# Two FFN ends of a two-layer diffusion backbone on one Trainium2 core: the last product's operands placed ahead of norm steps, the second end pinned to source order, and four residual buffers

## The chip, the cores and the metric

The kernel runs on one core of one Trainium2 chip. The metric is the device time of one execution in microseconds (us); a row of runs is given by its median. The engines are named as in the profile: PE is TensorE, DVE is VectorE, ACT is ScalarE, POOL is GpSimd, SP is SyncE, which issues most of the loads and stores. All arithmetic is float32; a matmul of two float32 operands is done as three passes over their high and low parts.

## The reference, cut to what matters

Two layers run over 512 latent tokens and 256 context tokens of 1024 columns. Each layer has a mixer and a SwiGLU FFN, and each of the two is wrapped in the same way:

```python
def _rms(x, gain, eps=1e-6):
    y = x * lax.rsqrt(jnp.mean(x * x, axis=-1, keepdims=True) + eps)
    return y * gain

def _swiglu(h, w_gate, w_up, w_down):
    return (jax.nn.silu(h @ w_gate) * (h @ w_up)) @ w_down
...
h_lat = _modulate(_rms(x_lat, norm_pre_ffn[l]), m_lat[3], m_lat[4])
x_lat = x_lat + m_lat[5] * _rms(_swiglu(h_lat, w_gate[l], w_up[l], w_down[l]), norm_post_ffn[l])
```

`m_lat` are the six parts of `silu(c) @ mod_w[l] + mod_b[l]`. In layer 0 the context tokens go through the same steps. In layer 1 only the latent tokens do, and `x_lat` behind its FFN is the output.

## The kernel before

Tokens are handled in tiles of 128: t = 0 to 3 latent, 4 and 5 context. The FFN of layer 0 runs over six tiles in the order 4, 5, 0, 1, 2, 3, the one of layer 1 over the four latent tiles.

**The down product** (`down`, L1706) uses a scheme of seven block products in place of eight. Each product p runs over 11 row pairs of the weights in six groups: g0 holds one pair, g1 to g5 two each. `operands` (L1728) makes what one group needs: the weight block is loaded to `raw` (or lies in `t`), ScalarE casts it to its high part `wH` (L1755) and the activations to theirs, `two` or `aH` (L1756); VectorE subtracts to get the low parts, `wL` (L1757), `two` again or `aL` (L1758). `two` has two places and `aH`/`aL` is the third, so they come round every three groups; `wH` and `wL` have four buffers. `ahead(3)` keeps three groups' operands made in advance. TensorE then takes, for each of nh token tiles, three matmuls per row pair: wH by the high part, wL by the high part, wH by the low part; every matmul is recorded at L355. Layer 0 has nh = 3, layer 1 has nh = 2.

The last product (p = 6, called "12") takes its last three groups g3, g4, g5 tile by tile: first all three for tile i = 0, then for i = 1, and so on. When a product has ended for a tile, VectorE adds it to the tile's sum `y` (L1798).

**The end of a tile** is `post_pre` (L1508), a generator that runs in steps. It loads the residual `xr` (L1512); ScalarE squares `y` and sums it up (L676, to `junk` and `sq`) and VectorE makes `pn` = y times the gate row `gv` (L746); next VectorE makes `ms` (L666) and GpSimd `rs` = ms to the power -0.5 (L668); then VectorE makes xr = pn * rs + xr (L755) and SP stores it. In layer 0 the norm of the next mixer follows: a Square of xr, `ms`, `rs`, and `dg`, the identity times rs (L689). From xr and dg of a pair of tiles TensorE makes the transposed tiles `hT` (in four `turn` steps), ScalarE scales them to `hf` (L727) and casts them (L734), VectorE makes their low parts (L735). That is h1, the input of the next mixer.

`later` (L1527) files such a generator with a count that begins two behind that of the one before, and `tick` (L1532) takes one step of the one with the smallest count. Product 5 files the ends of the first nh tiles; product 6 calls `tick` once for each group and tile (L1828) and files the others. In layer 1 the very last tile (3) has its own `final` (L2117): two halves with own sums of squares, tile `xl`.

**Who sets the order.** A scheduler puts each engine's instructions in order. Matmuls are pinned to program order in these stretches. In layer 0, `order_from` (L1546) marks the beginning of product 6, and `order_to` (L1549) makes each instruction of ScalarE and VectorE between that mark and its call wait for the one before it in the source, so that these two engines run in source order. In layer 1 nothing does.

Behind the first FFN the first part of the next mixer, the value product `nat` with its operands, begins in the same stretch (`values`, L2049): `value` (L2040) loads a weight unit to `raw` (three buffers), ScalarE casts it, VectorE makes its low part (L769, L770). The unit called `wx` is needed only for the second half of the columns. Then the modulation of layer 1 is summed up from rows of mod_w (`mraw`, `macc`, L579 to L597), and TensorE sums it over partitions (`mod_acc`).

Of the kernel before, what the change touches and what calls it, by code (L numbers as in the profile page):

```python
# [316 lines left out]
class Net:  # L317
# [353 lines left out]
    def sumsq(self, src, junk=None, ss=None):  # L671
        if junk is None:
            junk = self.wp.tile([P, D], BF16, tag="mraw", bufs=2, name="junk")[:, : src.shape[-1]]
        if ss is None:
            ss = self.sm.tile([P, 1], F32, tag="ss", name="ss")
        self.nc.scalar.activation(junk, src, AF.Square, accum_out=ss)  # L676
        return ss
# [830 lines left out]
    def post_pre(self, pp, y, t, gvs, xsrc, xdst, nxt, cuts):  # L1508

        nc = self.nc  # L1510
        xt = pp.tile([P, D], F32, tag="xt", bufs=4 if nxt and isinstance(nxt[2], Split) else 2, name=f"xr{t}")
        nc.sync.dma_start(out=xt, in_=xsrc(t))  # L1512

        def store(c):
            nc.sync.dma_start(out=xdst(t)[:, c], in_=xt[:, c])

        yield from self.post_norm(y, xt, gvs[0 if t < LT else 1], cuts, xdst and store)
        if nxt is not None:
            A, B, h = nxt
            yield from self.pre_norm(pp, t, xt, A, B, h)  # L1520
# [5 lines left out]

    def later(self, steps):  # L1527

        self.steps.append([self.steps[-1][2] + 2 if self.steps else 0, steps, 0])
        self.steps[-1][2] = self.steps[-1][0]  # L1530
# [175 lines left out]
    def down(self, l, fp, qp, rp, xp, quad, early, tiles, n, ending, finish):  # L1706
# [93 lines left out]
        for p, (name, where) in enumerate(seven):  # L1800
            order = [(g, i) for g in range(ng) for i in range(nh)]
            if p == 6:
                tail = ng - 3
                order = [(g, i) for g, i in order if g < tail] + [(g, i) for i in range(nh) for g in range(tail, ng)]
            if p == 6 and not l:
                self.order_from()
            for at, (g, i) in enumerate(order):
# [19 lines left out]
                if p == 6:  # L1827
                    self.tick()  # L1828
                    if begin and (g, i) == (tail + 1, 0):
                        begin(0, 0)  # L1830
                    if begin and i and g > tail:
                        self.turn_step()
                    if begin and g >= tail and i == nh - 1:
                        begin(0, g - tail + 1)
# [13 lines left out]
                elif name == "S3":  # L1848
                    nc.scalar.copy(y1[:, low], b)
                    plus(y1[:, high], b, ALU.subtract)  # L1850
                elif name == "22":
                    plus(y1[:, low], b)
                    self.later(end(y1, t1))
                    if l and i == nh - 1:
                        close = final(dp, y0, t0)
                else:
                    plus(y0[:, low], b)
                    if l and i == nh - 1:
                        close()
                    else:  # L1860
                        self.later(end(y0, t0))
        self.pinned = pinned
        yield follow

    def run(self):
# [170 lines left out]
        def ending(dp):  # L2036
# [12 lines left out]
            def values():  # L2049
# [12 lines left out]
                for c in range(2):  # L2062
                    for x, t in enumerate(order):
# [18 lines left out]
                        if c == 0 and x == 3:  # L2082
                            self.order_to(*self.latest)
                            value(1, 0)
                        if c or x > 2:
# [18 lines left out]
        def ending(dp):  # L2104
# [12 lines left out]
            def final(pool, y, t):  # L2117

                halves = [slice(512 * i, 512 * i + 512) for i in range(2)]
                xt = ep.tile([P, D], F32, tag="xt", bufs=2, name="xl")  # L2120
                nc.sync.dma_start(out=xt, in_=xat(x1)(t))
# [10 lines left out]
                def close():  # L2132
# [4 lines left out]
                    for c in halves:  # L2137
                        nc.vector.scalar_tensor_tensor(xt[:, c], tmp[:, c], rs, xt[:, c], op0=ALU.mult, op1=ALU.add)
                        nc.sync.dma_start(out=dst(t)[:, c], in_=xt[:, c])

                return close
# [58 lines left out]
```

## Time and profile before

| | us |
|---|---|
| median of 3 runs | 1691.47 |
| lowest and highest run | 1688.34, 1691.84 |
| profiled execution, its own time | 1689.01 |
| its span, first to last instruction | 1686.9 |
| product 6 of the first FFN on TensorE begins | 885.66 |
| product 6 of the second FFN on TensorE begins | 1660.49 |
| TensorE busy | 1646.0 (98%) |
| VectorE busy | 1309.3 (78%) |
| ScalarE busy | 920.0 (55%) |

A row of a timeline gives start, duration, engine, line, operation, output <- inputs, shapes, a count, and in brackets how long the engine was idle before it and what ended that. The names of buffers stand without their numbers, so that `xr` is that of any tile. The last line of a program is that of its closing instructions.

### The profile page before, as it was taken

What the parts mean: (1) busy time and instruction counts of PE and PEld (TensorE: products, weight loads), DVE (VectorE), ACT (ScalarE), POOL (GpSimd) and SP (SyncE); (2) the same over time, 40 slices, a digit from 0 to 9 for tenths busy, and PEclk for the clock granted to TensorE, in tenths of its full rate; (3) what the DMA queues carried; (4) which work ended last, traced back from release to release, by engine and by line L of the source; (5) the groups of instructions that cost most, each with busy time, mean ns of one, the idle gap of its engine ahead of it and who ended that gap; (6) DMA issues with size and microseconds to landing.
All of it is one profiled execution on the core that took longest, in us unless ns stands there. A gap on an engine that the chain in (4) does not pass through costs nothing.

```text
span 1686.9 us, 32540 instructions
## 1 busy us (share of the span) xinstructions
PE 1646.0 (98%) x13407; PEld 1481.6 (88%) x13407; DVE 1309.3 (78%) x2105; ACT 920.0 (55%) x1560; POOL 124.4 (7%) x129
## 2 busy tenths in 40 slices
PE   7999998999999999999999999999999999999997
PEld 5889987888999999998887888888888899999875
DVE  4889768875898988878667548788774599987987
ACT  4745567836543443445447436566664565555654
POOL 1004210011000000003102000000000100000221
PEclk9999999999999999999999999999999999999999
DMA  9651002164243444348625542121124333333793
GB/s 329 192 155 41 2 27 101 51 211 152 85 140 102 148 149 140 113 149 175 131 91 197 177 125 61 51 64 39 52 65 149 125 113 114 112 101 101 190 198 137
DMA packets 184736, 204.79 MB, mean 121 GB/s; under 512 B 7142, under 2 KB 141836, under 8 KB 184588
## 3 DMA queue, kind: packets, MB, share of 16 engines
q1 hardware_dynamic: 173632, 181.82, 34.4%
q0 software_dynamic: 9024, 17.30, 5.9%
q10 hardware_dynamic: 1932, 3.59, 0.6%
q8 instruction: 105, 1.72, 0.4%
q14 instruction: 43, 0.35, 0.1%
HBM read 193.23 MB, written 9.46 MB: 120 GB/s over the span
## 4 chain that ended last, share of the span: by engine, by line
PE 83%; DVE 8%; ACT 4%; DMA 3%; issue 2%; POOL 1%; DVEq 0%; SPq 0%; POOLq 0%; ACTq 0%
PE nat L355 12%; PE a L355 11%; PE ff L355 8%; PE E L355 8%; PE x L355 7%; PE oproj L355 6%; PE b L355 4%; PE D L355 4%; PE o L355 4%; PE fq L355 3%; PE gqk L355 2%; PE pearly L355 2%; PE S L355 2%; PE poh L355 1%; PE attO L355 1%
## 5 line engine op out<-in xcount | busy, mean ns | idle before, releaser
L355 PE MATMUL nat<-wH,x 128*128 128x256 f32 (+2 forms) x968 | 225.4, 321 | 3.0 <-ACT x L734 2.6
L355 PEld LDWEIGHTS nat<-wH,x 128*128 128x128 f32 x968 | 162.2, 190 | 19.2 <-ACT x L734 3.7
L824 ACT CAST wH<-raw 128x1024 fp32r<-128x1024 f32 x120 | 125.4, 1054 | 94.7 <-DVE raw L849 31.7
L825 DVE TENSOR_TENSOR wL<-raw,wH 128x1024 fp32r<-128x1024 f32 x120 | 145.6, 1220 | 20.4 <-ACT wH L824 19.9
L355 PE MATMUL nat<-wL,x 128*128 128x256 f32 (+2 forms) x484 | 153.4, 317 | 0.3 <-DVE wL L770 0.3
L770 DVE TENSOR_TENSOR wL<-raw,wH 128x1024 fp32r<-128x1024 f32 (+1 forms) x83 | 98.7, 1197 | 46.7 <-ACT wH L769 45.8
L355 PE MATMUL ff<-x,wH 128*128 128x512 f32 (+1 forms) x512 | 127.7, 340 | 0.0
L668 POOL TENSOR_TENSOR rs<-ms,neghalf 128x1 f32<-128x1 f32 (+2 forms) x62 | 66.5, 1077 | 783.3 <-DVE ms L666 783.2
L769 ACT CAST wH<-raw 128x1024 fp32r<-128x1024 f32 (+1 forms) x83 | 85.0, 1036 | 69.8 <-PE ff L355 19.8
L355 PE MATMUL oproj<-wH,x 128*128 128x512 f32 x320 | 102.2, 395 | 0.6 <-ACT x L1290 0.6
L597 DVE SCALAR_TENSOR_TENSOR macc<-mraw,scT,macc 128x1024 f32<-128x1024 f32 x70 | 88.2, 1279 | 13.8 <-DMA mraw<-in_mod_w_dram 13.6
L355 PEld LDWEIGHTS nat<-wL,x 128*128 128x128 f32 x484 | 92.1, 190 | 6.0 <-DVE wL L770 0.7
L355 PEld LDWEIGHTS ff<-x,wH 128*128 128x128 f32 x512 | 87.3, 190 | 10.0
L355 PE MATMUL x<-wH,two 128*128 128x512 f32 x280 | 90.5, 392 | 0.9 <-DVE y L1798 0.7
L976 ACT COPY qkh<-arr 128x512 f32<-128x512 f32 x112 | 70.2, 644 | 36.2 <-DVE arr L981 32.1
L1723 POOL DMA_DIRECT2D t<-in_ffn_w_down_dram x36 | 41.8, 1225 | 648.0 <-DVE wL L1757 610.7
L355 PE MATMUL ff<-x,wL 128*128 128x256 f32 (+1 forms) x256 | 86.2, 337 | 0.0
L849 DVE TENSOR_TENSOR raw<-raw 128x512 f32<-128x512 f32 x120 | 82.7, 689 | 2.8
L981 DVE TENSOR_TENSOR arr<-arr,f 128x512 f32<-128x512 f32 x112 | 74.1, 686 | 1.9 <-ACT qkh L976 0.3
L355 PE MATMUL E<-x,wH 128*128 128x384 f32 (+1 forms) x320 | 70.9, 311 | 0.0
L355 PEld LDWEIGHTS oproj<-wH,x 128*128 128x128 f32 x320 | 59.5, 188 | 12.8 <-ACT x L1290 1.2
L355 PE MATMUL a<-x,dH 128*128 128x384 f32 (+1 forms) x320 | 70.4, 309 | 0.2 <-ACT early L897 0.2
(420 smaller groups left out, 4544.6 us busy)
## 6 DMA issues: line engine op xcount, KB each, us to landing
mraw<-in_mod_w_dram SPq DMA_DIRECT2D x80, 512.0 KB, 4.4
raw<-in_ffn_w_gate_dram SPq DMA_DIRECT2D x44, 512.0 KB, 4.9
raw<-in_ffn_w_up_dram SPq DMA_DIRECT2D x44, 512.0 KB, 4.3
raw<-in_odd_w_in_dram SPq DMA_DIRECT2D x40, 512.0 KB, 3.7
t<-in_ffn_w_down_dram POOLq DMA_DIRECT2D x30, 512.0 KB, 7.8
raw<-in_ffn_w_down_dram SPq DMA_DIRECT2D x28, 512.0 KB, 7.5
mraw<-in_mod_w_dram SPq DMA_DIRECT2D x32, 256.0 KB, 6.0
raw<-in_even_w_in_dram SPq DMA_DIRECT2D x16, 512.0 KB, 3.9
```

What stands on the lines that cost most here:

```text
L355: return self.pin(self.nc.tensor.matmul(*a, **k))
L597: nc.vector.scalar_tensor_tensor(a, u, w, a, op0=ALU.mult, op1=ALU.add)
L668: nc.gpsimd.tensor_tensor(rs, ms, self.neghalf.to_broadcast([P, w]), op=ALU.pow)
L769: nc.scalar.copy(H[:, :m], raw[:, :m])
L770: nc.vector.tensor_tensor(L[:, :m], raw[:, :m], H[:, :m].bitcast(F32), op=ALU.subtract)
L824: self.nc.scalar.copy(H, f)
L825: self.nc.vector.tensor_tensor(L, f, H.bitcast(F32), op=ALU.subtract)
L849: add = lambda o, x, y: nc.vector.tensor_tensor(o, x, y, op=ALU.add)
L976: nc.scalar.copy(qkv[:, :, :, half, :], dst)
L981: nc.vector.tensor_tensor(dst, dst, tb, op=ALU.mult)
L1723: add = lambda o, src: self.pin(nc.gpsimd.dma_start(out=o, in_=src, accum_op=ALU.add))
```

## The change

Four things are changed.

1. In product 6, `tick` is no longer called at group g2 (`tail - 1`), but for g2's first tile in layer 0; at (g3, tile 0) it is called three times in layer 0 and twice in layer 1, in place of once.
2. The marks for source order are set in layer 1 too, and `close` of the last tile now returns its last Square and its last VectorE instruction, up to which source order holds. `later` has a gap of 0 in layer 1, so that the ends of two tiles take their steps in turn.
3. The tile `xt` of the residuals has four buffers in layer 1's FFN end, in place of two.
4. In layer 0, what the unit wx issues comes behind the last VectorE instruction of h1.

```diff
@@ -673,7 +673,7 @@
             junk = self.wp.tile([P, D], BF16, tag="mraw", bufs=2, name="junk")[:, : src.shape[-1]]
         if ss is None:
             ss = self.sm.tile([P, 1], F32, tag="ss", name="ss")
-        self.nc.scalar.activation(junk, src, AF.Square, accum_out=ss)
+        self.squared = self.nc.scalar.activation(junk, src, AF.Square, accum_out=ss)
         return ss
 
     def pre_norm(self, pool, t, xt, A, B, h):
@@ -1508,7 +1508,7 @@
     def post_pre(self, pp, y, t, gvs, xsrc, xdst, nxt, cuts):
 
         nc = self.nc
-        xt = pp.tile([P, D], F32, tag="xt", bufs=4 if nxt and isinstance(nxt[2], Split) else 2, name=f"xr{t}")
+        xt = pp.tile([P, D], F32, tag="xt", bufs=2 if nxt and isinstance(nxt[2], Forms) else 4, name=f"xr{t}")
         nc.sync.dma_start(out=xt, in_=xsrc(t))
 
         def store(c):
@@ -1524,9 +1524,9 @@
         while len(self.turns) > left:
             self.turns.pop(0)()
 
-    def later(self, steps):
-
-        self.steps.append([self.steps[-1][2] + 2 if self.steps else 0, steps, 0])
+    def later(self, steps, gap=2):
+
+        self.steps.append([self.steps[-1][2] + gap if self.steps else 0, steps, 0])
         self.steps[-1][2] = self.steps[-1][0]
 
     def tick(self, n=1):
@@ -1802,7 +1802,7 @@
             if p == 6:
                 tail = ng - 3
                 order = [(g, i) for g, i in order if g < tail] + [(g, i) for i in range(nh) for g in range(tail, ng)]
-            if p == 6 and not l:
+            if p == 6:
                 self.order_from()
             for at, (g, i) in enumerate(order):
                 if p == 5 and g == ng - 2 and i == 0:
@@ -1825,7 +1825,8 @@
                 if all(x != g for x, _ in order[at + 1 :]):
                     ready.pop((p, g))
                 if p == 6:
-                    self.tick()
+                    if g != tail - 1 or i == 0 and not l:
+                        self.tick((2 if l else nh) if (g, i) == (tail, 0) else 1)
                     if begin and (g, i) == (tail + 1, 0):
                         begin(0, 0)
                     if begin and i and g > tail:
@@ -1850,15 +1851,15 @@
                     plus(y1[:, high], b, ALU.subtract)
                 elif name == "22":
                     plus(y1[:, low], b)
-                    self.later(end(y1, t1))
+                    self.later(end(y1, t1), 0 if l else 2)
                     if l and i == nh - 1:
                         close = final(dp, y0, t0)
                 else:
                     plus(y0[:, low], b)
                     if l and i == nh - 1:
-                        close()
+                        self.order_to(*close())
                     else:
-                        self.later(end(y0, t0))
+                        self.later(end(y0, t0), 0 if l else 2)
         self.pinned = pinned
         yield follow
 
@@ -2081,7 +2082,8 @@
                         self.nc.scalar.copy(fi[:, t, 512 * c : 512 * c + 512], pt[:, :512])
                         if c == 0 and x == 3:
                             self.order_to(*self.latest)
-                            value(1, 0)
+                            with self.tc.issue_after(self.latest[1].ins):
+                                value(1, 0)
                         if c or x > 2:
                             mod(2 if c or x == 3 else 3)
                 self.pinned = False
@@ -2117,7 +2119,7 @@
             def final(pool, y, t):
 
                 halves = [slice(512 * i, 512 * i + 512) for i in range(2)]
-                xt = ep.tile([P, D], F32, tag="xt", bufs=2, name="xl")
+                xt = ep.tile([P, D], F32, tag="xt", bufs=4, name="xl")
                 nc.sync.dma_start(out=xt, in_=xat(x1)(t))
                 tmp = pool.tile([P, D], F32, name="pl")
                 ss = pool.tile([P, 2], F32, name="sl")
@@ -2135,8 +2137,9 @@
                     nc.vector.tensor_reduce(s, ss, axis=AX.X, op=ALU.add)
                     rs = self.rstd(s, D)
                     for c in halves:
-                        nc.vector.scalar_tensor_tensor(xt[:, c], tmp[:, c], rs, xt[:, c], op0=ALU.mult, op1=ALU.add)
+                        r = nc.vector.scalar_tensor_tensor(xt[:, c], tmp[:, c], rs, xt[:, c], op0=ALU.mult, op1=ALU.add)
                         nc.sync.dma_start(out=dst(t)[:, c], in_=xt[:, c])
+                    return self.squared, r
 
                 return close
```

The first place is the end of the first FFN, VectorE, where g5's operands (`wL` and `aL` from `qb`) are made. The numbered xr is that of tile 5:

```order
 L1758 TENSOR_TENSOR two<-zy,two 128x768
 L689 TENSOR_SCALAR dg_9495<-ident,rs 128x128
+L1757 TENSOR_TENSOR wL<-raw,wH 128x1024
+L1758 TENSOR_TENSOR aL<-qb,aH 128x768
 L755 SCALAR_TENSOR_TENSOR xr_9451<-pn,rs,xr_9451 128x1024
 L746 TENSOR_TENSOR pn<-y_8479,gv_9347 128x1024
-L1757 TENSOR_TENSOR wL<-raw,wH 128x1024
-L1758 TENSOR_TENSOR aL<-qb,aH 128x768
 L666 TENSOR_SCALAR ms<-ss 128x1
 L666 TENSOR_SCALAR ms<-sq 128x1
```

The two low parts now stand ahead of xr of tile 5 and of the next tile's pn. ScalarE at the same place:

```order
 L1755 CAST wH<-raw 128x1024
 L1756 CAST two<-zy 128x768
+L1755 CAST wH<-raw 128x1024
+L1756 CAST aH<-qb 128x768
 L676 ACTIVATE junk,sq<-y_8479 128x1024
-L1755 CAST wH<-raw 128x1024
-L1756 CAST aH<-qb 128x768
 L676 ACTIVATE junk,ss<-xr_9451 128x1024
```

g5's two casts have moved ahead of one Square of y.

The second place is where wx's low part stood on VectorE, between tile 2's pn and the `ms` of tiles 1 and 2:

```order
 L1798 TENSOR_TENSOR y_8479<-y_8479,x_8500 128x512
 L746 TENSOR_TENSOR pn<-y_8479,gv_9347 128x1024
-L770 TENSOR_TENSOR wx<-raw,wx 128x1024
 L666 TENSOR_SCALAR ms<-ss 128x1
 L666 TENSOR_SCALAR ms<-sq 128x1
```

It now stands behind the last L735, just ahead of the first `macc`; its cast on ScalarE has not moved. On SP one load of the value product goes with it, into the loads of mod_w:

```order
 L1515 DMA x_96<-xr_9577 128x1024
-L768 DMA raw<-in_odd_w_in_dram 128x2x512 x3
+L768 DMA raw<-in_odd_w_in_dram 128x2x512 x2
 L1515 DMA x_96<-xr_9702 128x1024
 L1515 DMA x_96<-xr_9736 128x1024
 L579 DMA mraw_9940<-in_mod_w_dram 128x1024
 L579 DMA mraw_9942<-in_mod_w_dram 128x1024
+L768 DMA raw<-in_odd_w_in_dram 128x2x512
 L579 DMA mraw_9973<-in_mod_w_dram 128x1024
```

The third of three loads has moved behind two stores and two loads of mod_w.

The third place is VectorE in product 6 of the second FFN, behind g2's `aL`. Before, with xr of tiles 0 (17859) and 1 (17895):

```order
L746 TENSOR_TENSOR pn<-y_17126,gv_17797 128x1024
L666 TENSOR_SCALAR ms<-sq 128x1
L1757 TENSOR_TENSOR wL<-raw,wH 128x1024
L1758 TENSOR_TENSOR two<-qb,two 128x512
L755 SCALAR_TENSOR_TENSOR xr_17859<-pn,rs,xr_17859 128x1024
L746 TENSOR_TENSOR pn<-y_17126,gv_17797 128x1024
L1757 TENSOR_TENSOR wL<-raw,wH 128x1024
L1758 TENSOR_TENSOR two<-qb,two 128x512
L666 TENSOR_SCALAR ms<-sq 128x1
L1757 TENSOR_TENSOR wL<-raw,wH 128x1024
L1758 TENSOR_TENSOR aL<-qb,aH 128x512
L1798 TENSOR_TENSOR y_17126<-y_17126,x_17143 128x512
```

The same place with the change, where tile 1's xr is 17869:

```order
L746 TENSOR_TENSOR pn<-y_17126,gv_17797 128x1024 x2
L1757 TENSOR_TENSOR wL<-raw,wH 128x1024
L1758 TENSOR_TENSOR two<-qb,two 128x512
L666 TENSOR_SCALAR ms<-sq 128x1 x2
L1757 TENSOR_TENSOR wL<-raw,wH 128x1024
L1758 TENSOR_TENSOR two<-qb,two 128x512
L1757 TENSOR_TENSOR wL<-raw,wH 128x1024
L1758 TENSOR_TENSOR aL<-qb,aH 128x512
L755 SCALAR_TENSOR_TENSOR xr_17859<-pn,rs,xr_17859 128x1024
L755 SCALAR_TENSOR_TENSOR xr_17869<-pn,rs,xr_17869 128x1024
L1798 TENSOR_TENSOR y_17126<-y_17126,x_17143 128x512
L746 TENSOR_TENSOR pn<-y_17126,gv_17797 128x1024
```

Both pn come first, then the operands of g3, g4 and g5 with only the two small ms between them, then both xr. Behind these rows, xr of tile 2 stood last of all on VectorE, behind both halves of xl; now it stands ahead of the last tile's y. On ScalarE both Squares of tiles 0 and 1 now stand ahead of g3's cast; before, the first stood behind it and the second behind g3's `two`. On SP tile 1's residual is loaded ahead of g4's and g5's weights, tile 2's right behind them, and the two stores of xl come last.

## The prediction

> **What bounds the kernel now.** The page comes first: its span, and the chain that ended last.
>
> ```profile
> span 1686.9 us, 32540 instructions
> ...
> PE 83%; DVE 8%; ACT 4%; DMA 3%; issue 2%; POOL 1%; DVEq 0%; SPq 0%; POOLq 0%; ACTq 0%
> ```
>
> TensorE carries the chain, so a change pays only where TensorE waits, or behind its last matmul. The change touches the last product of each FFN; the timelines of these two stretches come next. First TensorE at the end of the first FFN (start, duration, and in brackets the idle time before it with what ended it):
>
> ```profile
> 898.58 0.39 PE L355 MATMUL x<-wH,aH 128*128 128x512 f32 x1
> 900.53 0.50 PE L355 MATMUL x<-wL,aH 128*128 128x512 f32 x1 [1.56 <-DVE wL L1757]
> 901.39 0.50 PE L355 MATMUL x<-wH,aL 128*128 128x512 f32 x1 [0.37 <-DVE ms L666]
> ...
> 905.18 1.05 PE L355 MATMUL hT<-dg,xr 128*128 128x128 f32 x8
> ```
>
> Group g5's second and third matmul wait for its two low parts. At TensorE's pace (0.227 us a matmul) the third would start at 899.03 and not at 901.39: 2.36 us are lost, some 2.45 with the slower pace behind a wait. Next, where TensorE waits again in this stretch, and VectorE and ScalarE around both places:
>
> ```profile
> 922.98 0.94 PE L355 MATMUL hT<-dg,xr 128*128 128x128 f32 x6 [0.92 <-DVE dg L689]
> 923.67 0.48 PE L355 MATMUL nat<-wH,x 128*128 128x512 f32 x1
> ```
>
> ```profile
> 896.40 0.29 DVE L689 TENSOR_SCALAR dg<-ident,rs 128x128 f32<-128x128 f32 x1 [0.44 <-POOL rs L668]
> 896.92 1.28 DVE L755 SCALAR_TENSOR_TENSOR xr<-pn,rs,xr 128x1024 f32<-128x1024 f32 x1 [0.23 <-POOL rs L668]
> ...
> 899.25 1.22 DVE L1757 TENSOR_TENSOR wL<-raw,wH 128x1024 fp32r<-128x1024 f32 x1
> 900.39 0.95 DVE L1758 TENSOR_TENSOR aL<-qb,aH 128x768 fp32r<-128x768 f32 x1
> ...
> 903.04 0.29 DVE L689 TENSOR_SCALAR dg<-ident,rs 128x128 f32<-128x128 f32 x1 [0.44 <-POOL rs L668]
> ...
> 919.50 1.22 DVE L746 TENSOR_TENSOR pn<-y,gv 128x1024 f32<-128x1024 f32 x1
> 920.63 1.22 DVE L770 TENSOR_TENSOR wx<-raw,wx 128x1024 fp32r<-128x1024 f32 x1
> 921.77 0.14 DVE L666 TENSOR_SCALAR ms<-ss 128x1 f32<-128x1 f32 x1
> ```
>
> ```profile
> 895.84 0.84 ACT L1756 CAST aH<-qb 128x768 fp32r<-128x768 f32 x1 [0.21 <-PE x L355]
> ...
> 898.24 1.06 ACT L676 ACTIVATE junk<-xr 128x1024 bf16<-128x1024 f32 x1 [1.56 <-DVE xr L755]
> ...
> 912.16 1.03 ACT L727 ACTIVATE hf<-hT,modcol,aff 128x256 f32<-128x256 f32 x2 [0.64 <-PE hT L355]
> ```
>
> VectorE does a norm step (xr from 896.92, and a pn) before g5's operands, although ScalarE's second half for them, aH, stands ready from 896.68. At the end of the second FFN the same shows on TensorE once, and then VectorE has the end:
>
> ```profile
> 1660.49 0.39 PE L355 MATMUL x<-wH,two 128*128 128x512 f32 x1
> ...
> 1670.34 0.51 PE L355 MATMUL x<-wL,two 128*128 128x512 f32 x1 [1.29 <-DVE wL L1757]
> ```
>
> ```profile
> 1663.27 1.22 DVE L746 TENSOR_TENSOR pn<-y,gv 128x1024 f32<-128x1024 f32 x1
> ...
> 1678.05 0.69 DVE L1798 TENSOR_TENSOR y<-y,x 128x512 f32<-128x512 f32 x1 [0.89 <-PE x L355]
> ...
> 1681.99 1.28 DVE L755 SCALAR_TENSOR_TENSOR xr<-pn,rs,xr 128x1024 f32<-128x1024 f32 x1
> ```
>
> ```profile
> 1663.24 0.61 ACT L1756 CAST two<-qb 128x512 fp32r<-128x512 f32 x1
> ```
>
> ```profile
> 1654.60 3.38 SPq L1724 DMA_DIRECT2D raw<-in_ffn_w_down_dram  x2
> ...
> 1678.51 0.32 SPq L1512 DMA_DIRECT2D xr<-x  x1
> 1681.44 1.00 SPq L2139 DMA_DIRECT2D out_dram<-xl  x2
> 1683.30 0.33 SPq L1515 DMA_DIRECT2D out_dram<-xr  x1
> ```
>
> The very last step is token tile 2's xr. Its residual is loaded only at 1678.51, since two buffers serve four tiles, and its store, issued at 1683.30, ends the program 3.6 us later.
>
> **The change, part by part.** VectorE starts an instruction some 0.08 us before the one ahead of it ends (899.25, 1.22 long, then 900.39), so I count 1.13 us for 1024 columns, 0.87 for 768, 0.60 for 512, 1.20 for xr.
>
> *First FFN, operands ahead.* After dg (896.40) wL now runs 896.61 to 897.83, aL 897.74 to 898.70. TensorE wants them at 898.81 and 899.03: both waits go, and TensorE is some 2.45 us earlier at the next group. What is late next: xr and pn stand behind the operands (898.61 and 899.81), and the Square of xr on ScalarE moves from 898.24 to 899.93 and ends at 901.1. The value unit's cast stands behind that Square, its low part (1.22) behind the cast, and dg, at 903.04 before, comes at 903.2. TensorE's first hT needs that dg: it gets there near 902.7 and goes on at about 903.5, where it went on at 905.18 before: 1.7 us are kept. The Square of y, which now waits behind aH's cast (895.84, itself waiting for TensorE), ends by 897.7, and pn wants it at 899.81: nothing.
>
> *First FFN, wx.* ScalarE's hf at 912.16 had waited for hT, so it moves with TensorE, by 1.8. Behind it the casts and low parts of the value units follow, so that pn (919.50) comes at 917.67, 1.83 earlier. Then wx, which held VectorE from 920.63 to 921.77, is gone from here: ms moves by 1.83 + 1.13 = 2.96, from 921.77 to 918.8, and the dg on which TensorE waited 0.92 us comes at 919.68. TensorE, held about half a microsecond by the last of those low parts (an estimate from the same steps), reaches this hT at 919.8. Both meet, and nat (923.67) starts 2.97 us earlier. **First term: 2.97 us.** wx's low part now stands behind the last split of h1:
>
> ```profile
> 947.05 0.69 DVE L735 TENSOR_TENSOR x<-hf,x 128x512 fp32r<-128x512 f32 x1 [1.58 <-ACT x L734]
> ```
>
> ```profile
> L355 PEld LDWEIGHTS nat<-wx,x x36: 186/188/189, 955.8 to 985.3; 128*128 128x128 f32 x36
> ```
>
> Made by 949 and wanted at 955.8 on before's clock, it costs nothing by itself. The fourth value unit's load now waits for it (its buffer is wx's raw tile), and the modulation loads queue behind it on SP; that is the rival below.
>
> *Second FFN, source order.* On ScalarE both Squares now stand ahead of g3's cast: the first takes the place where `two` stood (1663.24 is when the first Square had ended), the second ends its sum at 1664.4. g3's cast ends at 1665.34, its `two` at 1665.86, g4's at 1667.33, g5's at 1668.80. VectorE: pn 1663.27, pn 1664.42, wL 1665.55, two 1666.68, two ms, wL 1667.41, two 1668.54, wL 1669.14, aL 1670.27 to 1670.95. TensorE reaches g3 at 1667.30 (30 matmuls of 0.227 behind 1660.49), g4 at 1668.66, g5 near 1670.5; it waits 0.2 to 0.4 us for g4's low part and ends near 1676.1, not 1678.03. That alone is not the gain, because VectorE is late next. GpSimd's square root does not get in between:
>
> ```profile
> 894.04 2.84 POOL L668 TENSOR_TENSOR rs<-ms,neghalf 128x1 f32<-128x1 f32 x2 [4.67 <-DVE ms L666]
> ...
> 1664.70 2.00 POOL L668 TENSOR_TENSOR rs<-ms,neghalf 128x1 f32<-128x1 f32 x1 [31.44 <-DVE ms L666]
> ...
> 1677.31 0.55 POOL L668 TENSOR_TENSOR rs<-ms,neghalf 128x1 f32<-128x1 f32 x1 [4.22 <-DVE ms L666]
> ```
>
> Alone it takes 0.55 us (1677.31). Behind VectorE's tensor_tensor instructions it takes 2.00 and ends about 0.4 after the last of them. So the first rs, asked for at 1667.5, comes at 1671.36. Then xr 1671.39, xr 1672.59, y 1673.79, pn 1674.5, ms 1675.7, rs 1676.5, xr 1676.57, and y of the last tile at 1677.77, where it was 1678.05: 0.28 earlier, as VectorE runs in order. From here on the steps are the same: the two half stores of xl go out 0.28 earlier, the second at 1681.82 (of the two at 1681.44 it is the last third of a microsecond, 1682.10). The issues by line give the time to landing:
>
> ```profile
> out_dram<-xr SPq DMA_DIRECT2D x3, 512.0 KB, 2.6
> ...
> out_dram<-xl SPq DMA_DIRECT2D x2, 256.0 KB, 2.1
> ```
>
> A half tile lands 2.1 us after its issue, at 1683.9, where the last whole tile landed at 1683.30 + 2.6 = 1685.9; the end moves by 2.0, from 1686.9 to 1684.9. **Second term: 2.0 us**, 0.3 from VectorE, the rest because xr and its full store no longer come last: four buffers let all residuals load at 1654 to 1658.
>
> One row is missing: whether the second rs gets in while the first xr begins at the same moment. In the pair at 894.04 the second rs ended 0.52 behind the first (dg 896.40, xr 896.92), with the short dg beside it: no delay. With a whole xr beside it, it could end 0.4 behind xr: 0.5 later. I take no delay, nearest to that pair.
>
> The Trainium skill, "SBUF — State Buffer", section "SBUF: two separate sides", says that VectorE with two SBUF inputs and GpSimd share one port pair, which whoever starts first holds for its whole instruction. The 2.00 us agree with it. By it either rs or xr would wait here, so the second term would be 1.5 rather than 2.0.
>
> *Loads.* The extra residual load (512 KB) goes ahead of g4's and g5's weights on SP. In a stretch of the first FFN in which the DMA engines were full, the core moved (last two columns: share and GB/s)
>
> ```profile
> 880.00:890.00 10.00, 10.00 (x46) 8.28 (x45) 6.70 (x10) 6.16 (x8) 0.56 (x1) 1.00 0.96 372
> ```
>
> so I estimate 1.4 us for it. g5's weights, issued at 1657.6 (the second of 1654.60), are wanted at 1667.2. Hidden.
>
> **Sum.** 2.97 + 2.0 = 5.0 us. The profiled execution took 1689.01 us (span 1686.9 and 2.1 around it), so it would take 1684.0. The median of the three runs, 1691.47, lies 2.46 above it; less 5.0, it gives **1686.5**.
>
> **Rivals.**
>
> *The first FFN gives it back.* dg at 903.2 is no earlier than before. If ScalarE's chain behind it (hf, casts, Squares) doesn't move up with TensorE, only wx's 1.13 us reach the dg at 922.64. For it: VectorE was the releaser in all of these waits. Against it: hf waited 0.64 for TensorE. Then 1.1 + 2.0 = 3.1: 1688.4.
>
> *The second FFN gives nothing.* VectorE has been the bound, and pn of tile 1 and both Squares now stand ahead of three groups. If gv or a Square lands 2 us later, y of the last tile does too, and it eats the 2.0: 1688.5.
>
> *The port*, as above: 4.5, 1687.0.
>
> *The modulation loads become the bound, and it is slower.* While the value product runs, VectorE adds up rows of mod_w as they land, and TensorE reads the sum:
>
> ```profile
> 983.32 1.06 PE L355 MATMUL mod_acc<-macc,one 128*32 128x512 f32 x8
> ```
>
> ```profile
> DVE macc L597 <- DMA mraw<-in_mod_w_dram: 9.3, 7, 2.4
> ```
>
> ```profile
> 979.45 1.28 DVE L597 SCALAR_TENSOR_TENSOR macc<-mraw,scT,macc 128x1024 f32<-128x1024 f32 x1 [1.70 <-DMA mraw<-in_mod_w_dram]
> ```
>
> The sum is ready at 980.73, 2.6 us ahead. wx pushes its beginning back by 1.1 beside TensorE's gain, and the added load in the queue by some 1.4: 0.1 of slack is left. If each of the seven waits for a load grows by one load of 1.4 us, TensorE stands 9.7 us: 4.7 us slower, 1696.2. It decides from 5.1 us of added waiting. Against it: one load moves into this stretch, not seven.
>
> *It does little*: the order was already forced by buffers, within 1 us of before. The rows show the low parts waiting for nothing but VectorE's turn, which speaks against it.
>
> **How the numbers follow.** Forecast 0.50, port 0.15, first FFN gives back 0.15, second FFN gives nothing 0.11, little 0.05, slower 0.04. A measurement of this kernel can tell about 0.2%, 3.4 us, from no change: forecast and port are over it, the next three within. That is 0.65, 0.31, 0.04. The runs of before lie 3.5 us apart, the lowest 3.1 under the median, so the range goes from 1683.3 (5.0 and the lowest run) to 1690.5 (little, 1 us gained); only the slower rival is outside it, and what the scatter adds.
>
> **What will show it.** Right: no wait of TensorE at g5 in the first FFN; its first hT about 1.7 us earlier, with a new wait for dg of half a microsecond or more; nat behind the second hT 3.0 earlier; TensorE's last matmul about 1.9 earlier against that, but y of the last tile only 0.3; xl last on VectorE. Wrong: nat behind the second hT less than 2 us earlier; a wait at mod_acc; y of the last tile later relative to the product's start; a gv that lands later.

## The result, and the profile after

The changed kernel takes 1683.48 us (median of 5 runs, 1682.4 to 1685.94), the kernel before 1691.29 us (5 runs beside it): a ratio of 0.996, with a 95% interval of 0.995 to 0.9971. In a second comparison, of the same two kernels later, it was 0.996 again (0.9947 to 0.9973). The two medians lie 7.8 us apart; by the ratio it is 6.8, with an interval of 4.9 to 8.5, and the forecast was 5.0 saved.

The profiled execution took 1683.48 us, with a span of 1681.5, 5.4 less than before. From the page, the span and the shares of the chain that ended last:

```profile
span 1681.5 us, 32537 instructions
...
PE 85%; DVE 7%; ACT 3%; DMA 3%; issue 1%; POOL 0%; ACTq 0%; DVEq 0%; POOLq 0%
```

TensorE carries slightly more of the chain, VectorE slightly less. Now TensorE at the end of the first FFN, in the timeline (the first three rows are the first three of g5's six matmuls for the first tile):

```profile
897.66 0.39 PE L355 MATMUL x<-wH,aH 128*128 128x512 f32 x1
897.88 0.39 PE L355 MATMUL x<-wL,aH 128*128 128x512 f32 x1
898.11 0.39 PE L355 MATMUL x<-wH,aL 128*128 128x512 f32 x1
...
901.74 0.38 PE L355 MATMUL hT<-dg,xr 128*128 128x128 f32 x2
902.60 0.94 PE L355 MATMUL hT<-dg,xr 128*128 128x128 f32 x6 [0.48 <-DVE dg L689]
...
918.99 1.12 PE L355 MATMUL hT<-dg,xr 128*128 128x128 f32 x8
919.86 0.47 PE L355 MATMUL nat<-wH,x 128*128 128x512 f32 x1
```

The waits of 1.56 and 0.37 us at g5 are gone: its matmuls follow each other at 0.227 us. In their place stands a wait of 0.48 for dg in the first hT, behind two of its eight matmuls, and the wait of 0.92 at the later hT, just ahead of nat, is gone too. VectorE around both places:

```profile
895.48 0.29 DVE L689 TENSOR_SCALAR dg<-ident,rs 128x128 f32<-128x128 f32 x1 [0.44 <-POOL rs L668]
895.68 1.22 DVE L1757 TENSOR_TENSOR wL<-raw,wH 128x1024 fp32r<-128x1024 f32 x1
896.82 0.95 DVE L1758 TENSOR_TENSOR aL<-qb,aH 128x768 fp32r<-128x768 f32 x1
897.68 1.28 DVE L755 SCALAR_TENSOR_TENSOR xr<-pn,rs,xr 128x1024 f32<-128x1024 f32 x1
...
901.12 1.22 DVE L770 TENSOR_TENSOR wL<-raw,wH 128x1024 fp32r<-128x1024 f32 x1 [0.73 <-ACT wH L769]
902.27 0.28 DVE L689 TENSOR_SCALAR dg<-ident,rs 128x128 f32<-128x128 f32 x1
...
916.82 1.22 DVE L746 TENSOR_TENSOR pn<-y,gv 128x1024 f32<-128x1024 f32 x1
917.96 0.14 DVE L666 TENSOR_SCALAR ms<-ss 128x1 f32<-128x1 f32 x1
```

The first dg stands at 895.48 where it stood at 896.40. Product 6 already begins 0.92 earlier (884.74 for 885.66), and so does the low part in front of this dg (894.09 for 895.01), so these 0.92 us are none of the change's doing, and every distance is taken from this dg. At the end of the second FFN, VectorE:

```profile
1664.46 0.21 DVE L666 TENSOR_SCALAR ms<-sq 128x1 f32<-128x1 f32 x2
1664.58 1.22 DVE L1757 TENSOR_TENSOR wL<-raw,wH 128x1024 fp32r<-128x1024 f32 x1
1665.72 0.68 DVE L1758 TENSOR_TENSOR two<-qb,two 128x512 fp32r<-128x512 f32 x1
...
1667.45 0.68 DVE L1758 TENSOR_TENSOR aL<-qb,aH 128x512 fp32r<-128x512 f32 x1
1668.06 2.47 DVE L755 SCALAR_TENSOR_TENSOR xr<-pn,rs,xr 128x1024 f32<-128x1024 f32 x2
...
1673.22 1.28 DVE L755 SCALAR_TENSOR_TENSOR xr<-pn,rs,xr 128x1024 f32<-128x1024 f32 x1 [0.73 <-POOL rs L668]
1674.42 0.68 DVE L1798 TENSOR_TENSOR y<-y,x 128x512 f32<-128x512 f32 x1
...
1677.03 1.42 DVE L2140 SCALAR_TENSOR_TENSOR xl<-pl,rs,xl 128x512 f32<-128x512 f32 x2 [0.73 <-DMA out_dram<-xr]
```

xl is now last on VectorE, and all three xr stand ahead of the last y. (The wait ahead of xl is put down to a store, but what VectorE waits for behind ms, 1676.14, is the rs below, done at 1676.99.) GpSimd and SP in the same stretch:

```profile
1664.76 2.05 POOL L668 TENSOR_TENSOR rs<-ms,neghalf 128x1 f32<-128x1 f32 x2 [35.37 <-DVE ms L666]
...
1676.44 0.55 POOL L668 TENSOR_TENSOR rs<-ms,neghalf 128x1 f32<-128x1 f32 x1 [3.25 <-DVE ms L666]
```

```profile
1651.07 0.90 SPq L1512 DMA_DIRECT2D xr<-x  x2
...
1655.03 0.58 SPq L1512 DMA_DIRECT2D xr<-x  x1
1669.36 5.51 SPq L1515 DMA_DIRECT2D out_dram<-xr  x3
1677.81 0.99 SPq L2141 DMA_DIRECT2D out_dram<-xl  x2
```

The loads of all three residuals are issued by 1655.6, and the program ends with two half stores where a whole one stood.

To read all the runs together, the span is cut at places that every kernel has: from the first dg to nat behind the later hT (the first FFN's end), from there to the start of product 6 of the second FFN (in it lie only wx's small parts and, in e7 and e8, the moved weight loads), and from that start to the last y and to the end of the span. In microseconds, each from one profiled execution:

| kernel | dg to nat | nat to product 6 | product 6 to last y | product 6 to end |
|---|---|---|---|---|
| before | 27.27 | 736.82 | 17.56 | 26.38 |
| before, again | 27.25 | 736.61 | 17.59 | 26.40 |
| changed | 24.38 | 737.63 | 16.93 | 23.96 |
| changed, again | 24.39 | 736.41 | 17.11 | 24.15 |
| e1 first FFN alone | 24.37 | 737.13 | 17.53 | 26.34 |
| e2 second FFN alone | 27.26 | 736.93 | 16.92 | 23.95 |
| e3 wx as before | 25.54 | 737.06 | 16.93 | 23.95 |
| e4 order, two buffers | 24.41 | 735.81 | 26.48 | 33.52 |
| e5 four buffers alone | 27.29 | 738.58 | 17.92 | 24.96 |
| e6 xr beside rs | 24.40 | 737.36 | 18.03 | 25.07 |
| e7 adds later | 24.38 | 736.65 | 16.98 | 24.01 |
| e8 both of these | 24.40 | 736.27 | 17.91 | 24.94 |
| e7, again | 24.39 | 735.89 | 16.92 | 23.95 |

The first FFN gives 2.89 us and the second 2.42, together 5.3. Kernels with the same edit repeat the two end stretches within 0.06 us, but for the second end of the changed kernel's second trace, 0.2 longer, where VectorE waits 0.18 us longer for gv; the long stretch between them, and the time ahead of the first dg (895.35 to 899.20), scatter by 2.8 and 3.9 us. (In e6's 899.20 some 1.7 us are the granted clock's, by an estimate: it is 0.66 on average between 105 and 110 us there and 1.00 in the changed kernel, and 0.34 of 5 us is 1.7.) So the times of two executions can differ by more than the change is worth: the runs of before alone lie between 1686.62 and 1694.44 us.

### The profile page after: what moved, and what is told of

It reads as the page before. It is cut to its first block, busy times and chain, and to the rows that moved or that the text cites. A ratio compares the mean times of both kernels' runs of the same rounds, so it can differ in the third digit from the quotient of the medians.

```text
span 1681.5 us, 32537 instructions
## 1 busy us (share of the span) xinstructions
PE 1644.6 (98%) x13407; PEld 1481.0 (88%) x13407; DVE 1309.8 (78%) x2105; ACT 917.5 (55%) x1560; POOL 121.4 (7%) x129
## 4 chain that ended last, share of the span: by engine, by line
PE 85%; DVE 7%; ACT 3%; DMA 3%; issue 1%; POOL 0%; ACTq 0%; DVEq 0%; POOLq 0%
PE nat L355 13%; PE a L355 12%; PE ff L355 8%; PE E L355 8%; PE x L355 7%; PE oproj L355 6%; PE o L355 4%; PE D L355 4%; PE b L355 4%; PE fq L355 3%; PE gqk L355 2%; PE pearly L355 2%; PE S L355 2%; PE poh L355 1%; PE attO L355 1%
## 5 line engine op out<-in xcount | busy, mean ns | idle before, releaser
L355 PE MATMUL b<-x,wH 128*128 128x384 f32 (+1 forms) x320 | 70.5, 309 | 0.0
```

The costliest lines, as they stand in the source:

```text
L355: return self.pin(self.nc.tensor.matmul(*a, **k))
```

## The experiments

The theory is the prediction's: two independent terms, operands ahead and wx away in the first FFN, and in the second the buffers, which take xr and its full store from the end, with a little of VectorE's order. One thing in the new trace spoke against plain adding: of the 2.89 us that TensorE was ahead at nat, 0.81 were missing at product 6. It waits in the second FFN's product that the trace calls q: first to last start of its 66 matmuls took 16.35 us, where 65 steps of 0.2266 are 14.73. One of these waits is

```profile
1608.40 0.49 PE L355 MATMUL q<-wL,aH 128*128 128x512 f32 x1 [0.24 <-DVE wL L1757]
```

and from the start at 1607.14 to the one at 1609.34 four steps take 2.20 us where 0.91 would do. ScalarE, in front of VectorE there, waits for weights:

```profile
1602.00 1.05 ACT L1755 CAST wH<-raw 128x1024 fp32r<-128x1024 f32 x1 [4.01 <-DMA raw<-in_ffn_w_down_dram]
...
1606.04 1.05 ACT L1755 CAST wH<-raw 128x1024 fp32r<-128x1024 f32 x1 [2.47 <-DMA raw<-in_ffn_w_down_dram]
```

So a rival stood beside the theory: the weight loads of the second FFN take back part of whatever the first one gains.

### e1: the first FFN alone

Against the kernel before:

```diff
-                    self.tick()
+                    if l or g != tail - 1 or i == 0:
+                        self.tick(nh if not l and (g, i) == (tail, 0) else 1)
...
-                            value(1, 0)
+                            with self.tc.issue_after(self.latest[1].ins):
+                                value(1, 0)
```

> Only the first FFN is changed (low parts of g5 ahead of the norm steps, wx behind h1); the second FFN stays as before, with two residual buffers. Theory A (the terms simply add up): nat behind the second hT comes 2.9 us earlier against dg of the first norm step than in before, and product 6 of the second FFN begins 2.9 us earlier too; time 2.9 us under before. Theory B (the second FFN's down product is bound by its weight loads): nat comes 2.9 us earlier, but TensorE then waits some 0.8 us for a low part wL in the product recorded as q, 48 us ahead of product 6, and only 2.1 us are left at product 6 and at the end. Theory C (the first FFN gives nothing by itself): under 1 us at nat.

Measured: 0.9974 of before (0.9965 to 0.9984), 4.4 us by the ratio with 2.7 to 5.9 as its interval. From dg to nat 24.37 us, 2.90 less than before. The first term stands. TensorE loses 1.6 us in q (16.31), as the rival says, and the long stretch is 0.31 longer than before's, between theory A (nothing) and B (0.8).

### e2: the second FFN alone

Against the changed kernel:

```diff
-                    if g != tail - 1 or i == 0 and not l:
-                        self.tick((2 if l else nh) if (g, i) == (tail, 0) else 1)
+                    if not l or g != tail - 1:
+                        self.tick(2 if l and (g, i) == (tail, 0) else 1)
...
-                            with self.tc.issue_after(self.latest[1].ins):
-                                value(1, 0)
+                            value(1, 0)
```

> Only the second FFN's end is changed (source order, gap 0, no tick at g2, four buffers). The recorded working: y of the last tile 0.28 us earlier against the start of product 6, the end 2.0 us earlier against that start. By the trace of the changed kernel it should be 0.63 at y and 2.4 at the end. If the port held GpSimd's second root back, 1.5. At q there should be no new wait, since TensorE comes there no earlier than before.

Measured: 0.9984 (0.9975 to 0.9993), 1.2 to 4.2 us. From product 6 to the last y 0.64 us less than before, to the end 2.43 less: the trace of the changed kernel to a hundredth. The product of the ratios of e1 and e2 is 0.9958, beside the changed kernel's 0.996: the parts add. And in q:

```profile
1611.55 0.49 PE L355 MATMUL q<-wL,aH 128*128 128x512 f32 x1 [0.24 <-DVE wL L1757]
```

the same wait (1.6 us lost in q, 16.31), in a kernel with the first FFN of before. No new wait was expected there; that there is one speaks against the rival.

### e3: wx as before

Against the changed kernel:

```diff
-                            with self.tc.issue_after(self.latest[1].ins):
-                                value(1, 0)
+                            value(1, 0)
```

> The changed kernel, with the unit wx issued where it was before. The recorded working gives wx 1.13 us of the first term: nat behind the second hT 1.1 us later than in the changed kernel, with a wait of TensorE for dg of about 0.9. Rival: TensorE comes to this hT with dg ready anyway or is held by the value product's own low parts, and wx is worth under 0.3 us. Third: since the weight loads of the second FFN take 0.8 us back anyway, nat is 1.1 us later but the start of product 6 only 0.3.

Measured: 0.9971 (0.9959 to 0.9982), not to be told from the changed kernel. In the trace it can be told. TensorE, and VectorE ahead of it:

```profile
920.83 0.94 PE L355 MATMUL hT<-dg,xr 128*128 128x128 f32 x6 [0.92 <-DVE dg L689]
921.52 0.47 PE L355 MATMUL nat<-wH,x 128*128 128x512 f32 x1
```

```profile
918.48 1.22 DVE L770 TENSOR_TENSOR wx<-raw,wx 128x1024 fp32r<-128x1024 f32 x1
919.62 0.15 DVE L666 TENSOR_SCALAR ms<-ss 128x1 f32<-128x1 f32 x1
...
920.49 0.28 DVE L689 TENSOR_SCALAR dg<-ident,rs 128x128 f32<-128x128 f32 x1 [0.67 <-POOL rs L668]
```

The wait of 0.92 is back to the hundredth, and nat comes 25.54 us behind the first dg, 1.16 later than in the changed kernel. So wx is worth 1.16 of the first term, and the operands ahead 1.73. The third theory, that only 0.3 of it would be left at product 6, can't be read from a stretch that scatters by more.

### e4: source order with two buffers

Against the changed kernel:

```diff
-        xt = pp.tile([P, D], F32, tag="xt", bufs=2 if nxt and isinstance(nxt[2], Forms) else 4, name=f"xr{t}")
+        xt = pp.tile([P, D], F32, tag="xt", bufs=4 if nxt and isinstance(nxt[2], Split) else 2, name=f"xr{t}")
...
-                xt = ep.tile([P, D], F32, tag="xt", bufs=4, name="xl")
+                xt = ep.tile([P, D], F32, tag="xt", bufs=2, name="xl")
```

> The changed kernel with two residual buffers in the second FFN in place of four. xl and tile 0 hold both, so tile 1's residual loads only behind tile 0's store (1669.4 + 2.6 + 3.3 = 1675.3) and tile 2's behind tile 1's store (1676.5 + 2.6 + 3.3 = 1682.4). Theory A (source order makes every later y wait for these loads): the end some 9 us later than in the changed kernel, 1692 to 1694, slower than before. Theory B (the order alone is the gain, buffers only help): the last y as in the changed kernel and the end within 2 us of it.

Measured: 1.0019 (1.001 to 1.0028), slower than before, although its first FFN gains as the changed kernel's does. From product 6 to the end 33.52 us, 9.56 more than in the changed kernel. VectorE and SP:

```profile
1674.05 1.28 DVE L755 SCALAR_TENSOR_TENSOR xr<-pn,rs,xr 128x1024 f32<-128x1024 f32 x1 [6.05 <-DMA xr<-x]
1675.25 0.68 DVE L1798 TENSOR_TENSOR y<-y,x 128x512 f32<-128x512 f32 x1
...
1681.42 1.28 DVE L755 SCALAR_TENSOR_TENSOR xr<-pn,rs,xr 128x1024 f32<-128x1024 f32 x1 [4.12 <-DMA xr<-x]
1682.62 0.68 DVE L1798 TENSOR_TENSOR y<-y,x 128x512 f32<-128x512 f32 x1
```

```profile
1668.02 0.36 SPq L1515 DMA_DIRECT2D out_dram<-xr  x1
1670.67 0.34 SPq L1512 DMA_DIRECT2D xr<-x  x1
1675.36 0.34 SPq L1515 DMA_DIRECT2D out_dram<-xr  x1
1677.99 0.32 SPq L1512 DMA_DIRECT2D xr<-x  x1
```

Each of these residuals is loaded some 2.6 us behind the store of the one before it, and each xr waits for that load with the next tile's y queued behind it. Source order, with the ticks and the gap that go with it, costs 7.1 us against before; it needs the four buffers. (No run takes pinning, ticks and gap apart.)

### e5: four buffers alone

Against the kernel before:

```diff
-        xt = pp.tile([P, D], F32, tag="xt", bufs=4 if nxt and isinstance(nxt[2], Split) else 2, name=f"xr{t}")
+        xt = pp.tile([P, D], F32, tag="xt", bufs=2 if nxt and isinstance(nxt[2], Forms) else 4, name=f"xr{t}")
...
-                xt = ep.tile([P, D], F32, tag="xt", bufs=2, name="xl")
+                xt = ep.tile([P, D], F32, tag="xt", bufs=4, name="xl")
```

> The kernel before with four residual buffers in the second FFN's end and nothing else. The residuals then load early, and tile 2's xr stands ahead of the last y by the scheduler's own choice. Theory A (the recorded working: 0.3 us of the second term from VectorE's order, the rest from xr and its full store no longer being last): 1.7 to 2.1 us of the 2.43 us that the second FFN's part gives between the start of product 6 and the end. Theory B (the order carries it): under 0.5 us, since the xr that is now ahead of the last y pushes it back.

Measured: 0.9991 (0.9982 to 1.0), by time not to be told from before. From product 6 to the end 24.96 us, 1.42 less than before. VectorE:

```profile
1674.72 1.28 DVE L755 SCALAR_TENSOR_TENSOR xr<-pn,rs,xr 128x1024 f32<-128x1024 f32 x1 [0.44 <-POOL rs L668]
...
1678.69 1.28 DVE L755 SCALAR_TENSOR_TENSOR xr<-pn,rs,xr 128x1024 f32<-128x1024 f32 x1 [0.73 <-POOL rs L668]
1679.90 0.68 DVE L1798 TENSOR_TENSOR y<-y,x 128x512 f32<-128x512 f32 x1
```

Nearer to theory A than to B, under its lower end: tile 2's xr, now ahead of the last y, puts that y 0.36 us later (17.92 for 17.56) and the end keeps 1.42 of the 2.43. With four buffers, the order (pinning, ticks and gap) then adds 1.0: the last y goes from 17.92 to 16.92.

### e6: xr beside rs

Against the changed kernel:

```diff
-                    if g != tail - 1 or i == 0 and not l:
-                        self.tick((2 if l else nh) if (g, i) == (tail, 0) else 1)
+                    if l and g >= tail - 1:
+                        self.tick((1 if g == tail else 0) if i == 0 else 0 if g < tail else 2 if g == ng - 1 else 1)
+                    elif g != tail - 1 or i == 0:
+                        self.tick(nh if (g, i) == (tail, 0) else 1)
```

> The changed kernel with tile 1's xr moved on VectorE behind tile 2's ms, so that it runs while GpSimd makes tile 2's rs (in the changed kernel VectorE stands idle there for 0.73 us). Theory A (the two share a port, and VectorE starts first): rs takes about 1.6 us and ends some 0.4 us behind xr; the last y is at most 0.1 us earlier against the start of product 6. Theory B (no hindrance): rs takes 0.55 to 0.61 us, VectorE does not wait, the last y and the end come 0.5 us earlier.

Measured: 0.9975 (0.9967 to 0.9984); the last y and the end are 1.1 us later against product 6 than in the changed kernel, worse than either theory. VectorE and GpSimd:

```profile
1672.96 0.69 DVE L1798 TENSOR_TENSOR y<-y,x 128x512 f32<-128x512 f32 x1
1674.87 1.22 DVE L746 TENSOR_TENSOR pn<-y,gv 128x1024 f32<-128x1024 f32 x1 [1.22 <-ACT junk L676]
1676.01 0.14 DVE L666 TENSOR_SCALAR ms<-sq 128x1 f32<-128x1 f32 x1
1676.07 1.27 DVE L755 SCALAR_TENSOR_TENSOR xr<-pn,rs,xr 128x1024 f32<-128x1024 f32 x1
1677.79 1.28 DVE L755 SCALAR_TENSOR_TENSOR xr<-pn,rs,xr 128x1024 f32<-128x1024 f32 x1 [0.44 <-POOL rs L668]
```

```profile
1676.30 1.46 POOL L668 TENSOR_TENSOR rs<-ms,neghalf 128x1 f32<-128x1 f32 x1 [5.97 <-DVE ms L666]
```

On the port, theory A holds: xr began 0.23 us ahead of rs, and rs, 0.55 us alone, took 1.46 and ended at 1677.76, 0.42 behind xr's end at 1677.34. So nothing was won here by work of VectorE beside rs. The rest was overlooked: pn and the Squares' junk share two buffers, tile 1's pn holds one until its xr is done, and tile 2's pn waited 1.22 us for the Square to leave the other.

### e7 and e8: the accumulating loads spread out

GpSimd's queue loads some weight blocks so that they are added to what the tile `t` holds; these are the accumulating loads. Against the changed kernel:

```diff
-            v.tensor_tensor(L, src, H.bitcast(F32), op=ALU.subtract)
+            split = v.tensor_tensor(L, src, H.bitcast(F32), op=ALU.subtract)
...
-            elif name == "N3":
-                add(t3(i), B(1, 1, i))
-            elif name == "SN":
-                add(t(i), B(1, 0, i))
+            elif name == ("SN" if l else "N3"):
+                behind(add(t3(i), B(1, 1, i)), split)
+            if name == ("S3" if l else "SN"):
+                behind(add(t(i), B(1, 0, i)), split)
```

Here `behind` makes the load wait, in layer 1, for the low part named. e8 is e7 with e6's edit.

> The changed kernel with the accumulating weight loads of the second FFN spread out: those issued by GpSimd during the product recorded as q (loads of its own on SP) wait until the next product's low parts, and those of that product until the one behind it. Theory A (in q the transfers of both queues compete, so that raw lands late): the 0.75 us that TensorE waited in q in the changed kernel's trace, and ScalarE's waits of 4.0 and 2.5 us for raw there, go; the stretch from nat behind the second hT to product 6 is 736.8 us as in before, or less. Theory B (the waits at q come from something else): ScalarE still waits over 2 us for raw there. Theory C (the loads now come late in a later product): a new wait of TensorE there, longer than 0.75 us.

> The edits of the two kernels ahead of it together: tile 1's xr behind tile 2's ms, and the accumulating loads spread out. If both help, the sum, 1 us under the changed kernel; if the port hinders the first and the loads are not the cause, no difference to it.

Measured: e7 0.9962 (0.9949 to 0.9974), e8 0.9966 (0.9954 to 0.9979). TensorE loses nothing in q in either (14.73 us); nat to product 6 is 736.65 and 736.27. ScalarE waits there for weights once in e7, 3.01 us, where it did twice in the first trace of the changed kernel, 4.01 and 2.47. e8 has e6's later end (24.94). No new wait shows in the later products.

### The changed kernel, the kernel before and e7 once more

No edit; the three kernels ran on one chip.

> The changed kernel once more, for the 0.8 us that its trace lost between nat (behind the second hT) and product 6 of the second FFN. Theory A (scatter of when a weight load lands): the length of that stretch differs again, by some tenths up to 1 us, and the wait at q is longer, shorter or gone. Theory B (the change itself causes it, since TensorE now comes early to a load that is late): the same wait, 0.6 to 0.9 us in q, and a stretch of 737.6 us. The two ends: nat 24.4 us behind the first dg, the end 23.96 us behind the start of product 6, both as in the first trace.

> The kernel before once more, for the same reason. Theory A: it too can wait in q, and its stretch lies anywhere between 735.8 and 737.6 us. Theory B: 736.8 us and no wait in q, as in its first trace. The two ends: nat 27.27 us behind the first dg, the end 26.38 us behind the start of product 6.

> The changed kernel with the accumulating loads spread out, once more, beside a run of the changed kernel on the same chip. If spreading them takes the wait in q away: again no wait of TensorE in q, and a stretch of 736.3 to 736.7 us. If its absence was scatter: a wait as often as in the other kernels.

Measured, each against before: 0.996 (0.9947 to 0.9973), 1.0 (0.9992 to 1.0009) and 0.9956 (0.9944 to 0.9968). The changed kernel lost nothing in q this time, and took 736.41 us from nat to product 6, less than either trace of before. So the 0.81 us are scatter, not a price of the change: theory A. Of the ten traces with the loads as they were, five lose 1.35 to 1.62 us in q (the changed kernel, e1, e2, e5, e6), three 0.5 to 0.6 (before, twice, and e3) and two nothing (the changed kernel again, e4); e2 and e5 lose it with the first FFN of before.

What makes the scatter is shown less surely. With the accumulating loads spread out three traces of three lose nothing in q; if the edit did nothing, three drawn from these 13 would all be among the five without loss about once in 29. So the two queues' transfers may well compete there, as e7's theory A has it; this is argued and not shown. Spreading them would then be worth 0.9 us on average (the mean loss of the ten). In time e7 is not to be told from the changed kernel, 0.9956 beside 0.996 on one chip.

## Why the prediction was right

Each time below is on before's clock (0.92 us added in the first FFN).

**Operands ahead.** Right, to a tenth. The two waits went. dg, forecast at 903.2 and no earlier than before, came at 903.19; TensorE, forecast to go on at 903.5, went on at 903.52, with a wait of 0.48 ("half a microsecond or more"), two matmuls of that hT being done before it. As forecast, ScalarE had the Square of xr ahead of the value unit's cast, and VectorE waited 0.73 us for that cast (901.12): what is late next.

**The rival that the first FFN gives it back** fell: pn came at 917.74 (forecast 917.67) and ms at 918.88 (918.8), so ScalarE's chain did move up with TensorE.

**wx.** Forecast 1.13, 1.16 by e3. nat stood at 920.78, forecast 920.70. The whole first term, forecast 2.97, is 2.86 to 2.90 in every kernel that has it. (The working has 1.7 us kept at the first hT and, without a reason, 1.8 at the hf behind it; the trace has 1.74 at that hf, 910.42 for 912.16.)

**The modulation loads**, the slower rival, did not come up: TensorE shows no wait at mod_acc, and its lead was 3.82 us there (979.50 for 983.32), 0.92 of it from before the change.

**The other rivals.** That the second FFN gives nothing fell by e2, 2.43 us by itself; gv came no later, since the first pl, which waits for it (y times gv, of the last tile), stands 1.34 us ahead of product 6 and stood 1.37 ahead. That the change does little fell by e1 and e2 together.

**Second FFN, VectorE's order.** The mechanism was right, the size not: 0.64 us at the last y, forecast 0.28. The step that failed is "the first rs, asked for at 1667.5, comes at 1671.36". I had it blocked until the last low part ended, as in before. In the trace both rs were done at 1666.81, ahead of aL's end (1668.13), so both xr followed aL at once, 10.57 us behind the start of product 6 where 10.90 was forecast. That is 0.33 of the missing 0.36. (It would be 0.5, but the low parts came 0.17 to 0.18 later than worked out.) (The rows of the two orders are in the last section.) TensorE's last matmul was 1.53 us earlier against product 6, forecast 1.9; it mattered to nothing, since VectorE came later.

**The buffers.** "0.3 from VectorE, the rest because xr and its full store no longer come last" has the right two parts. The second was right to a tenth: from the last y to the end it took 8.82 us before and 7.03 with the change, 1.79 less where 1.7 was forecast. But the parts are not independent. Those 7.03 stand in e4 and e5 too (7.04): the order or the buffers alone take xr and its full store from the end. They differ at the last y, which comes 0.36 us later with the buffers alone, 8.92 later with the order alone and 0.64 earlier with both. So alone the buffers give 1.42 (e5), alone the order takes 7.1 (e4), together they give 2.43. The working had named the reason for four buffers, but not that source order turns a late residual into a wait of every later y.

**The port.** The second term was 2.4 and not 1.5, but that does not test the rival, because its condition did not come up: by the time both xr ran, nothing of GpSimd was under way. Where the two do meet, in e6, the cost is there. The Trainium skill, "SBUF — State Buffer", section "SBUF: two separate sides", has whoever starts first hold the port pair for its whole instruction; e6 agrees (rs 1.46 us, ending 0.42 behind xr).

**The sum.** 2.89 + 2.42 = 5.3 us by the traces, forecast 5.0. The runs gave more, 6.8 by the ratio, with 5.3 inside the intervals of both comparisons. The measured 1683.48 us lies 3.0 under the forecast of 1686.5 and only 0.2 above the lower end of the range, which had been drawn from the scatter of three runs; that it lies inside is partly luck. Of the rest, part is that the median of the runs of before lay between 1689.8 and 1691.5 from one comparison to the next. Another part goes with the mean granted clock that each run lists: in the second comparison it was 0.997 or less in 10 of before's 17 runs and in 1 of the changed kernel's 6, and without these the means lie 5.1 us apart, with them 6.4. Why before's runs show it more often stays open; nothing in the two end stretches points to a further gain.

## What to carry to other kernels

Ahead of a last product, place what TensorE still needs before the norm steps that only the end needs, and count what the moved steps make late next; that gave the size to a tenth in the first FFN. A wait taken over from the old trace is not safe: in the second FFN the rs that stood blocked before came early once the order around it had changed. Before pinning an engine to source order, give every transfer that an instruction in that order waits for a buffer of its own: the same order gained 1.0 us with four buffers and cost 7.1 with two. Where a change is worth a few tenths of a per cent, cut the span at places that every kernel has and compare the pieces, since the rest scatters: 2.8 us in one stretch here and 3.9 in another, for a change worth 5.3.

## What the runs showed of the hardware that was not expected

GpSimd's rs, when a VectorE instruction with two operands is under way, ends 0.41 to 0.42 us behind the end of such an instruction, but not always the last of a row. Before, asked for during wL, it ran on until 0.42 behind the `two` that followed (1664.70, 2.00 long):

```profile
1664.47 1.21 DVE L1757 TENSOR_TENSOR wL<-raw,wH 128x1024 fp32r<-128x1024 f32 x1
1665.60 0.68 DVE L1758 TENSOR_TENSOR two<-qb,two 128x512 fp32r<-128x512 f32 x1
```

In the changed kernel, with two rs in the queue, the first ended at 1666.22, 0.42 behind wL's end (1665.80), while the next `two` ran, and the second 0.41 behind that `two`, while the next wL ran:

```profile
1666.20 0.61 POOL L668 TENSOR_TENSOR rs<-ms,neghalf 128x1 f32<-128x1 f32 x1
```

Neither VectorE instruction was longer for it (0.68 and 1.22). Every other trace with this order, e2, e3, e4, e6, e7 and e8 and the repeats, shows the same two lengths within 0.01, and the traces with before's order (before again, e1, e5) the 2.00. What decides between the two is open.

The landing of weight loads in the second FFN differs from execution to execution: TensorE's 66 matmuls of q took 16.35 us in one trace of the changed kernel and 14.73 in the other, and ScalarE waited there for weights 4.01 and 2.47 us in the first, once and 1.68 in the second.
